# A GLA head's eight samples loaded, multiplied and normalised in one step instead of two of four

## The chip, the cores and the metric

One core of a Trainium2 chip runs the whole kernel. The metric is the device time of one execution in microseconds (us); lower is better. A core has five engines with a queue of instructions each: PE (matmul; its weight loads, PEld, overlap it), DVE (vector), ACT (scalar, activations), POOL and SP (here both mostly issue DMAs). An engine runs its queue in order, and waits on semaphores for the others.

## What is computed

The reference is one layer of a hybrid decoder: a gated linear recurrence (LRU) and gated linear attention (GLA) side by side, for a prompt of 2048 tokens and for eight samples of one token with states of their own. The change concerns the samples in GLA. For each of four heads, with a state `S` of 128 x 256 per sample:

```
S = exp(dl[:, :, 0, :])[..., None] * S + k^T v          # for one token
o = q S
o = o * lax.rsqrt(jnp.mean(o * o, axis=-1, keepdims=True) + EPS) * g_gla_norm
y_gla = o.reshape(Bn, T, D_GLA) * silu(zg)
```

The new states are an output, and `y_gla` goes, with the prompt's, into the output projection.

## The kernel before

The prompt is done in two halves of 1024 tokens; the second half carries the samples' eight columns as well. Within a half the heads follow in the order 3, 0, 1, 2. A head projects its values (matmuls L346 to L348, three for one product since operands are split in a high and a low part, and L661 to L663 for all other projections), then runs GLA over three segments of 384, 384 and 256 + 8 columns, in chunks of 128 tokens, and behind each head stands an LRU tile (L1315 to L1317 are its gates, with the convolution L1278 and the scan L1318 to L1334 around them).

A chunk of GLA goes like this. ACT rounds the transposed keys and the masked products (L1051 kTh, L1048 amh), DVE makes their low parts (L1052 kTl, L1049 aml). PE multiplies keys and values (L1068 to L1070, the last with kTl) and adds up the chunk's outputs in the one PSUM buffer po (L1072 to L1076). DVE copies them out (L1081), which frees po for the next L1072, and ACT sums their squares (L165). A segment's norm is a chain of small DVE steps (rsqrt, L147 to L153), then L1089 scales the outputs, L1162 transposes them on PE, and L1167 multiplies by gain and gate.

The samples of a head are done by `sample_state` and `sample_out`, four at a time. A group loads its value rows, copied to all 128 partitions (L1098), and its states (L1100), both issued from POOL into two buffers of 4 x 256 columns with the tag xt, of which there are just two. Per sample DVE puts the query into a zeroed tile (L1103 qm), ACT scales the state by the decay (L1104), and DVE adds key times value (L1105). Three units of work later PE multiplies the four queries by the four states (L1114: 32 rows of po for each sample), the states go out (L1115), and po is copied to the tile os (L1117). The second group, two units behind the first, needs the buffers of the first and so waits until its products are done; its products are added to os by DVE (L1119). Then follow the sum of squares, rsqrt, and the scale (L1124). The last segment's outputs for the samples are brought into place by L1164, beside L1162, which waits for L1124. `finish` holds that step back until the norm is in the program.

What stands where is not written by hand. Functions queue pieces of work with `after(units, fn)`; `tick()` counts units between pieces of projection and starts what is due. A scheduler then orders the instructions of each engine when the program is built, by its own estimates of time. On chip each engine follows that order.

Two raw buffers with the tag wr hold a head's unsplit value weights (`raw_values`, L333, on POOL), which L912 reads for the samples' values; near the end of the kernel two loads of another kind (L1960, SP) use them. A head's raw weights are read before its samples' states are loaded.

Of the kernel before, what the change touches and what calls it, by code (L numbers as in the profile page):

```python
# [8 lines left out]
F32 = mybir.dt.float32  # L9
F32R = mybir.dt.float32r  # L10
I32 = mybir.dt.int32
AF = mybir.ActivationFunctionType
OP = mybir.AluOpType

P = 128
# [4 lines left out]
NS = 8  # L20
H = 4
DK = 128
DV = 256
# [26 lines left out]
def dram(ap, off, pattern):  # L50
    return bass.AP(tensor=ap.tensor, offset=ap.offset + off, ap=pattern)
# [3 lines left out]
def hybrid_kernel(ctx, tc, i, o):  # L55
    nc = tc.nc
    V, S, G, PE, SP = nc.vector, nc.scalar, nc.gpsimd, nc.tensor, nc.sync
# [13 lines left out]
    vsd = dpool.tile([H, NS, DV], F32, tag="vsd", name="vsd")  # L71
# [11 lines left out]
    cp = p1.enter_context(tc.tile_pool(name="cp", bufs=1))  # L83
    hnp = p1.enter_context(tc.tile_pool(name="hnp", bufs=1))
    wp = p1.enter_context(tc.tile_pool(name="wp", bufs=2))
    xp = p1.enter_context(tc.tile_pool(name="xp", bufs=2))
# [22 lines left out]
    sc = cp.tile([P, KT, 32], F32, tag="sc", name="sc")  # L109
# [591 lines left out]
    def after(units, fn, gla=False, val=False):  # L701
        clock[1] += 1
        heapq.heappush(pend, (clock[0] + units, clock[1], fn, gla, val))
# [384 lines left out]
        for c in range(nch):  # L1088
            V.tensor_scalar(on[:, c], on[:, c], rs[:, c:c + 1], None, op0=OP.mult)  # L1089

    def sample_state(h, smp, b0, st, done):

        if b0 == 0:
            st[:] = [cp.tile([P, NS, 32], F32, tag="sc", name="qm"), gp.tile([P, DV], F32, tag="os", name="os")]
            V.memset(st[0], 0.0)
        qm = st[0]
        vb = xp.tile([P, 4, DV], F32, tag="xt", name="xt")
        G.dma_start(vb, dram(vsd, (h * NS + b0) * DV, [[0, P], [DV, 4], [1, DV]]))  # L1098
        s0 = xp.tile([P, 4, DV], F32, tag="xt", name="xt")
        G.dma_start(s0, i["state_gla"][0, b0:b0 + 4, h].rearrange("b k v -> k b v"))  # L1100
        for n in range(4):
            b = b0 + n
            V.tensor_copy(qm[:, b, b:b + 1], smp[:, 0, b:b + 1])  # L1103
            S.activation(s0[:, n], s0[:, n], AF.Copy, scale=smp[:, 2, b:b + 1])  # L1104
            V.scalar_tensor_tensor(s0[:, n], vb[:, n], smp[:, 1, b:b + 1], s0[:, n],  # L1105
                                   op0=OP.mult, op1=OP.add)
        after(3, lambda: sample_out(h, b0, st, s0, done), True)

    def sample_out(h, b0, st, s0, done):

        qm, os_ = st
        po = psum.tile([P, 512], F32, tag="o", name="po", bufs=1)[:, :DV]
        for n in (3, 0, 1, 2):
            PE.matmul(po[32 * n:32 * n + 32], qm[:, b0 + n], s0[:, n], start=True, stop=True)  # L1114
        G.dma_start(o[7][0, b0:b0 + 4, h].rearrange("b k v -> k b v"), s0)  # L1115
        if b0 == 0:
            V.tensor_copy(os_, po)  # L1117
            return
        V.tensor_tensor(os_, os_, po, op=OP.add)  # L1119
        ss = gp.tile([P, 4], F32, tag="oss2", name="oss2")  # L1120
        rs = gp.tile([P, 4], F32, tag="ors2", name="ors2")
        square_sum(xp, ss[:, :1], os_, P, DV)
        rsqrt(gp, rs[:, :1], ss[:, :1], 1, P, 1.0 / DV)
        V.tensor_scalar(os_, os_, rs[:, :1], None, op0=OP.mult)  # L1124
        done()

    def silu(z, ps):
        S.activation(z, ps, AF.Tanh, scale=0.5)  # L1128
# [41 lines left out]
    def gla_head(half, h, wv=None, ahead=None):  # L1170
# [4 lines left out]
        else:  # L1175
# [5 lines left out]
            v = values(half, h, w)  # L1181
            wk = weights(K0 + h * DK, DK)
            wq = weights(Q0 + h * DK, DK)
        prep, zs, os_, state = {}, {}, [None], []

        def chunks(s, c):

# [28 lines left out]
                return  # L1216
            gla_out(half, h, s, prep[s, "run"][1], os_[0] if s == 2 else None, [zs[s, 0], zs[s, 1]])

        def sample(smp, b0):
            sample_state(h, smp, b0, state, lambda: after(0.5, lambda: os_.__setitem__(0, state[1]), True))  # L1220

        pk = None
        if not wv:
# [18 lines left out]
                after(2 if h == HEADS[0] else 1, lambda: chunks(0, 0), True, True)  # L1242
            tick()
        if half == 1:
            after(1, lambda: sample(prep[2][3], 0), True)
            after(3, lambda: sample(prep[2][3], 4), True)
        if wv:
            modulate_samples(st, xsr)
            hn_sample()
# [807 lines left out]
    smp = {}  # L2057
# [201 lines left out]
```

## Time and profile before

| | us |
|---|---|
| three runs | 1453.64, 1453.55, 1456.39 (median 1453.64) |
| profiled execution | 1452.05 |
| its span | 1450.3 |
| L1104, one of 32 (ACT) | 0.50 |
| L1105, one of 32 (DVE) | 0.48 |
| L1114, landing of its states (L1100, median) | 5.9 |

The prediction quotes rows of the trace: start in us, duration in us, engine, line, operation, tiles (written tile <- read tiles), shape, and in brackets the idle time of that engine before the row with what ended it. A row with x2 or x4 covers that many instructions in a row (for the products, x8 counts the two passes of each). Rows of waits give engine, tile and line that waited, what it waited for, then us in total, times, and the longest. Line numbers are those of the kernel before, unless said otherwise.

### The profile page before, as it was taken

The numbers are of one execution on the slowest core, as the hardware profiler recorded it, in microseconds if no ns is written. First come the engines' busy times: TensorE is split into PE (matmuls) and PEld (weight loads), VectorE is DVE, ScalarE is ACT, GpSimd is POOL, SyncE is SP. The second block draws the span as 40 slices with busy tenths as digits, with TensorE's granted clock in tenths as the row PEclk, the third lists the DMA queues.
The fourth block names the chain that finished last, engine by engine and source line by source line (L and its number), as shares of the span: only waits on it lengthen the run. The fifth ranks groups of instructions, "written<-read, shape, count | busy, mean of one in ns | idle before, by whom it ended". The sixth has DMA issues, their size and how long they took to land. (4 is left out here: it accounts for less than half of the span.)

```text
span 1450.3 us, 23579 instructions
## 1 busy us (share of the span) xinstructions
PE 1425.6 (98%) x8741; PEld 1253.1 (86%) x8741; DVE 1051.2 (72%) x2477; ACT 690.0 (48%) x1251; POOL 220.5 (15%) x364
## 2 busy tenths in 40 slices
PE   8999999999999999999999999999999999999998
PEld 6888989899898988878999998999998887788886
DVE  5757658776676688955458687686888986688886
ACT  4644544662545358624354544535557522144342
POOL 0200111212122013100111321433210000000000
PEclk9999999999999999999999999999999999999999
DMA  9755775774665446667844665756672767694453
GB/s 329 267 185 175 259 264 196 251 243 156 200 217 192 160 175 213 204 224 236 293 153 154 201 205 163 244 188 203 213 256 77 279 223 273 229 361 135 135 173 116
DMA packets 161752, 305.33 MB, mean 211 GB/s; under 512 B 12962, under 2 KB 91458, under 8 KB 159197
## 3 DMA queue, kind: packets, MB, share of 16 engines
q1 hardware_dynamic: 106837, 217.39, 44.0%
q0 software_dynamic: 22752, 70.44, 14.3%
q10 hardware_dynamic: 32048, 16.00, 3.7%
q8 instruction: 69, 1.13, 0.3%
q14 instruction: 46, 0.38, 0.1%
HBM read 188.51 MB, written 115.33 MB: 210 GB/s over the span
## 5 line engine op out<-in xcount | busy, mean ns | idle before, releaser
L661 PE MATMUL acc<-hh,w 128*128 128x512 f32 (+3 forms) x1112 | 386.2, 347 | 1.3 <-DVE zs L1129 0.7
L663 PE MATMUL acc<-hh,w 128*128 128x512 f32 (+3 forms) x1112 | 375.6, 338 | 0.0
L662 PE MATMUL acc<-hl,w 128*128 128x512 f32 (+3 forms) x1112 | 375.3, 338 | 0.2 <-DVE hl L205 0.2
L661 PEld LDWEIGHTS acc<-hh,w 128*128 128x128 f32 x1112 | 209.3, 188 | 20.0 <-ACT tx L1318 0.9
L662 PEld LDWEIGHTS acc<-hl,w 128*128 128x128 f32 x1112 | 209.3, 188 | 17.2 <-DVE hl L205 0.5
L663 PEld LDWEIGHTS acc<-hh,w 128*128 128x128 f32 x1112 | 209.1, 188 | 16.8 <-issue 0.4
L1845 PE MATMUL acc<-w,a 128*128 128x512 f32 (+1 forms) x792 | 184.8, 386 | 0.0
L1845 PEld LDWEIGHTS acc<-w,a 128*128 128x128 f32 x792 | 146.8, 188 | 33.2 <-issue 3.4
L346 PE MATMUL acc<-w,hh 128*128 128x256 f32 (+1 forms) x508 | 144.9, 285 | 0.1
L347 PE MATMUL acc<-w,hh 128*128 128x256 f32 (+1 forms) x508 | 143.6, 283 | 0.0
L348 PE MATMUL acc<-w,hl 128*128 128x256 f32 (+1 forms) x508 | 143.6, 283 | 0.0
L1845 PE MATMUL tp<-w,a 128*128 128x512 f32 x564 | 136.0, 391 | 0.0
L1845 PEld LDWEIGHTS tp<-w,a 128*128 128x128 f32 x564 | 105.3, 188 | 26.8 <-issue 5.2
L346 PEld LDWEIGHTS acc<-w,hh 128*128 128x128 f32 x508 | 96.8, 191 | 1.3 <-ACT zs L1128 0.4
L348 PEld LDWEIGHTS acc<-w,hl 128*128 128x128 f32 x508 | 96.4, 190 | 0.0
L347 PEld LDWEIGHTS acc<-w,hh 128*128 128x128 f32 x508 | 95.9, 189 | 0.2
L1128 ACT ACTIVATE zs<-acc 128x512 f32<-128x512 f32 (+3 forms) x70 | 34.5, 492 | 107.4 <-PE acc L663 105.2
L1695 ACT CAST a<-s 128x512 fp32r<-128x512 f32 x61 | 36.5, 619 | 95.9 <-issue 36.6
L1278 DVE SCALAR_TENSOR_TENSOR cv<-xa,vecT,cv 128x512 f32<-128x512 f32 (+2 forms) x120 | 77.1, 645 | 6.0 <-ACT cv L1276 5.7
L1129 DVE SCALAR_TENSOR_TENSOR zs<-zs,acc 128x512 f32<-128x512 f32 (+3 forms) x70 | 38.6, 551 | 47.3 <-ACT zs L1128 47.2
L957 ACT CAST vh<-acc 128x256 fp32r<-128x256 f32 x56 | 20.5, 370 | 83.3 <-PE acc L348 70.0
L958 DVE TENSOR_TENSOR vl<-acc,vh 128x256 fp32r<-128x256 f32 x56 | 23.4, 420 | 43.1 <-ACT vh L957 43.0
(403 smaller groups left out, 2752.0 us busy)
## 6 DMA issues: line engine op xcount, KB each, us to landing
parts<-w SPq DMA_DIRECT2D x37, 1024.0 KB
w<-parts SPq DMA_DIRECT2D x28, 1024.0 KB
wr<-in_w_in_dram SPq DMA_DIRECT2D x38, 512.0 KB
a<-mixd SPq DMA_DIRECT2D x63, 256.0 KB
w<-wd SPq DMA_DIRECT2D x12, 1024.0 KB
w<-twd SPq DMA_DIRECT2D x20, 512.0 KB
mixd<-zs ACTq DMA_DIRECT2D x34, 256.0 KB
wada<-in_w_ada_dram SPq DMA_DIRECT2D x16, 512.0 KB
```

The source lines that it names most:

```text
L346: PE.matmul(ps, hh[:, kt, c], hi[:, kt % 4], start=kt == 0, stop=False)
L347: PE.matmul(ps, hh[:, kt, c], lo[:, kt % 4], start=False, stop=False)
L348: PE.matmul(ps, hl[:, kt, c], hi[:, kt % 4], start=False, stop=kt == KT - 1)
L661: PE.matmul(ps[:, :n], hi[:, kt], a, start=kt == 0, stop=False)
L662: PE.matmul(ps[:, :n], hi[:, kt], b, start=False, stop=False)
L663: PE.matmul(ps[:, :n], lo[:, kt], a, start=False, stop=kt == KT - 1)
L958: V.tensor_tensor(lo, ps[:, :DV], hi.bitcast(F32), op=OP.subtract)
L1128: S.activation(z, ps, AF.Tanh, scale=0.5)
L1129: V.scalar_tensor_tensor(z, z, 1.0, ps, op0=OP.add, op1=OP.mult)
L1278: V.scalar_tensor_tensor(cv[:, cq], xa[:, cq.start + k:cq.stop + k], cw[k], cv[:, cq], op0=OP.mult, op1=OP.add)
L1695: S.copy(t[:, 0, k], (low(t) if src is None else src)[:, k])
L1845: PE.matmul(ps, t[:, u, k], w[:, v, k, c], start=(q < 3 or ps is own) and (k, u, v) == (0, 0, 0), stop=(k, u) == (3, 1), skip_group_check= ...
```

## The change

`sample_state` is now called once per head, one unit behind the last segment's projections, and loads all eight samples: the first four into the xt buffers, the second four into the wr buffers. The scales of all eight follow each other. `sample_out` comes four units later (before: three, for each group) and multiplies all eight into one PSUM buffer: the first four start the sums, the second four add to them, which is the same as adding the two results since each product has rows of zeros for the other samples. One copy to os remains, the add is gone. The norm's end is told to `finish` as before, half a unit later.

```diff
@@ -1088,41 +1088,42 @@
         for c in range(nch):
             V.tensor_scalar(on[:, c], on[:, c], rs[:, c:c + 1], None, op0=OP.mult)
 
-    def sample_state(h, smp, b0, st, done):
-
-        if b0 == 0:
-            st[:] = [cp.tile([P, NS, 32], F32, tag="sc", name="qm"), gp.tile([P, DV], F32, tag="os", name="os")]
-            V.memset(st[0], 0.0)
-        qm = st[0]
-        vb = xp.tile([P, 4, DV], F32, tag="xt", name="xt")
-        G.dma_start(vb, dram(vsd, (h * NS + b0) * DV, [[0, P], [DV, 4], [1, DV]]))
-        s0 = xp.tile([P, 4, DV], F32, tag="xt", name="xt")
-        G.dma_start(s0, i["state_gla"][0, b0:b0 + 4, h].rearrange("b k v -> k b v"))
-        for n in range(4):
-            b = b0 + n
-            V.tensor_copy(qm[:, b, b:b + 1], smp[:, 0, b:b + 1])
-            S.activation(s0[:, n], s0[:, n], AF.Copy, scale=smp[:, 2, b:b + 1])
-            V.scalar_tensor_tensor(s0[:, n], vb[:, n], smp[:, 1, b:b + 1], s0[:, n],
-                                   op0=OP.mult, op1=OP.add)
-        after(3, lambda: sample_out(h, b0, st, s0, done), True)
-
-    def sample_out(h, b0, st, s0, done):
-
-        qm, os_ = st
+    def sample_state(h, smp, done):
+
+        qm = cp.tile([P, NS, 32], F32, tag="sc", name="qm")
+        V.memset(qm, 0.0)
+        s0 = []
+        for b0, pool, tag in ((0, xp, "xt"), (4, wp, "wr")):
+            vb, x = [pool.tile([P, 1088], F32, tag=tag, name=tag)[:, :4 * DV] if b0 else
+                     pool.tile([P, 4 * DV], F32, tag=tag, name=tag) for _ in range(2)]
+            vb, x = [y.rearrange("p (b v) -> p b v", v=DV) for y in (vb, x)]
+            G.dma_start(vb, dram(vsd, (h * NS + b0) * DV, [[0, P], [DV, 4], [1, DV]]))
+            G.dma_start(x, i["state_gla"][0, b0:b0 + 4, h].rearrange("b k v -> k b v"))
+            for n in range(4):
+                b = b0 + n
+                V.tensor_copy(qm[:, b, b:b + 1], smp[:, 0, b:b + 1])
+                S.activation(x[:, n], x[:, n], AF.Copy, scale=smp[:, 2, b:b + 1])
+                V.scalar_tensor_tensor(x[:, n], vb[:, n], smp[:, 1, b:b + 1], x[:, n],
+                                       op0=OP.mult, op1=OP.add)
+            s0.append(x)
+        after(4, lambda: sample_out(h, qm, s0, done), True)
+
+    def sample_out(h, qm, s0, done):
+
+        os_ = gp.tile([P, DV], F32, tag="os", name="os")
         po = psum.tile([P, 512], F32, tag="o", name="po", bufs=1)[:, :DV]
-        for n in (3, 0, 1, 2):
-            PE.matmul(po[32 * n:32 * n + 32], qm[:, b0 + n], s0[:, n], start=True, stop=True)
-        G.dma_start(o[7][0, b0:b0 + 4, h].rearrange("b k v -> k b v"), s0)
-        if b0 == 0:
-            V.tensor_copy(os_, po)
-            return
-        V.tensor_tensor(os_, os_, po, op=OP.add)
+        for m in range(2):
+            for n in (3, 0, 1, 2):
+                PE.matmul(po[32 * n:32 * n + 32], qm[:, 4 * m + n], s0[m][:, n], start=m == 0, stop=m == 1)
+        for m in range(2):
+            G.dma_start(o[7][0, 4 * m:4 * m + 4, h].rearrange("b k v -> k b v"), s0[m])
+        V.tensor_copy(os_, po)
         ss = gp.tile([P, 4], F32, tag="oss2", name="oss2")
         rs = gp.tile([P, 4], F32, tag="ors2", name="ors2")
         square_sum(xp, ss[:, :1], os_, P, DV)
         rsqrt(gp, rs[:, :1], ss[:, :1], 1, P, 1.0 / DV)
         V.tensor_scalar(os_, os_, rs[:, :1], None, op0=OP.mult)
-        done()
+        done(os_)
 
     def silu(z, ps):
         S.activation(z, ps, AF.Tanh, scale=0.5)
@@ -1181,7 +1182,7 @@
             v = values(half, h, w)
             wk = weights(K0 + h * DK, DK)
             wq = weights(Q0 + h * DK, DK)
-        prep, zs, os_, state = {}, {}, [None], []
+        prep, zs, os_ = {}, {}, [None]
 
         def chunks(s, c):
 
@@ -1216,8 +1217,8 @@
                 return
             gla_out(half, h, s, prep[s, "run"][1], os_[0] if s == 2 else None, [zs[s, 0], zs[s, 1]])
 
-        def sample(smp, b0):
-            sample_state(h, smp, b0, state, lambda: after(0.5, lambda: os_.__setitem__(0, state[1]), True))
+        def sample(smp):
+            sample_state(h, smp, lambda x: after(0.5, lambda: os_.__setitem__(0, x), True))
 
         pk = None
         if not wv:
@@ -1242,8 +1243,7 @@
                 after(2 if h == HEADS[0] else 1, lambda: chunks(0, 0), True, True)
             tick()
         if half == 1:
-            after(1, lambda: sample(prep[2][3], 0), True)
-            after(3, lambda: sample(prep[2][3], 4), True)
+            after(1, lambda: sample(prep[2][3]), True)
         if wv:
             modulate_samples(st, xsr)
             hn_sample()
```

In the changed kernel L1104 is L1105, L1105 is L1106, L1103 is L1104, L1114 is L1117, L1124 is L1125, and L1127 to L1245 move on by one (L1162 is L1163, L1164 is L1165, L1167 is L1168).

The new order shows in three places. First ACT in head 0, in the last segment's GLA, where the states of the first four (xt) were scaled. Before:

```order
L1011 ACTIVATE e<-xb 128x256
L1104 ACTIVATE xt<-xt,smp 128x256
L1012 ACTIVATE xb<-xb 128x256
L165 ACTIVATE junk,oss<-on 128x256
L1051 CAST kTh<-tp 128x384
L1048 CAST amh<-am 128x384
```

After, with wr the states of the second four:

```order
L1105 ACTIVATE xt<-xt,smp 128x256
L1012 ACTIVATE xb<-xb 128x256
L1105 ACTIVATE wr<-wr,smp 128x256 x4
L165 ACTIVATE junk,oss<-on 128x256
L1051 CAST kTh<-tp 128x384
L1048 CAST amh<-am 128x384
```

The four scales of the second group stand behind the exponential L1012 and ahead of the sum of squares and the two roundings of the chunk.

Second DVE in head 1, from the norm of the second segment (L1089) to the copy of a chunk's outputs (L1081). Before:

```order
L1089 TENSOR_SCALAR on<-on,ors 128x256 x3
L1103 COPY qm<-smp 128x1
L1105 SCALAR_TENSOR_TENSOR xt<-xt,smp 128x256
L1103 COPY qm<-smp 128x1 x4
L1167 SCALAR_TENSOR_TENSOR zs<-tp,gsc,zs 128x384
L1081 COPY on<-po 128x256
```

After:

```order
L1089 TENSOR_SCALAR on<-on,ors 128x256 x3
L1104 COPY qm<-smp 128x1 x2
L1106 SCALAR_TENSOR_TENSOR wr<-wr,smp 128x256
L1104 COPY qm<-smp 128x1
L1106 SCALAR_TENSOR_TENSOR wr<-wr,smp 128x256
L1104 COPY qm<-smp 128x1
L1106 SCALAR_TENSOR_TENSOR wr<-wr,smp 128x256
L1104 COPY qm<-smp 128x1
L1106 SCALAR_TENSOR_TENSOR wr<-wr,smp 128x256
L1168 SCALAR_TENSOR_TENSOR zs<-tp,gsc,zs 128x384
L1081 COPY on<-po 128x256
```

Four steps on the states of the second group stand there instead of one on the first.

Third PE in head 0, at the products and the LRU gates. Before, the second group of products:

```order
L661 MATMUL acc<-hh,w 128x264
L662 MATMUL acc<-hl,w 128x264
L663 MATMUL acc<-hh,w 128x264
L1114 MATMUL po<-xt,qm 32x256 x4
L1315 MATMUL acc<-xh,wg 128x264
L1316 MATMUL acc<-xl,wg 128x264
L1317 MATMUL acc<-xh,wg 128x264
```

After, the one place of all products, with the last 128x384 projections ahead of it:

```order
L661 MATMUL acc<-hh,w 128x384
L662 MATMUL acc<-hl,w 128x384
L663 MATMUL acc<-hh,w 128x384
L1117 MATMUL po<-xt,qm 32x256 x4
L1117 MATMUL po<-wr,qm 32x256 x4
L1315 MATMUL acc<-xh,wg 128x384
L1316 MATMUL acc<-xl,wg 128x384
L1317 MATMUL acc<-xh,wg 128x384
```

The products moved from behind the 128x264 projections of the head's last gate to ahead of them, and the group that stood among the 128x384 projections is gone.

## The prediction

> **What bounds the kernel now.** I read the busy times of the profile's page first, then PE's waits, then the granted clock by stretches around the longest wait, then the timelines of that place, engine by engine.
>
> ```profile
> PE 1425.6 (98%) x8741; PEld 1253.1 (86%) x8741; DVE 1051.2 (72%) x2477; ACT 690.0 (48%) x1251; POOL 220.5 (15%) x364
> ```
> ```profile
> PE po L1114 <- DVE xt L1105: 2.1, 1, 2.1
> PE acc L1315 <- DVE zs L1129: 1.4, 1, 1.4
> PE tp L1164 <- DVE os L1124: 0.8, 1, 0.8
> ```
>
> PE works 98% of the span, so only what takes work or a wait off PE counts, and any new wait of PE is paid in full. One of its longest waits is at the lines changed: L1114 waits once, 2.1 us, for the scaled states of L1105. The stretches around it (us, then PE, PEld, DVE, ACT, POOL busy, and the granted clock):
>
> ```profile
> 20.61:24.02 3.41, 1.47 (x32) 0.96 (x28) 2.19 (x7) 0.19 (x1) 0.00 (x0) 1.00 1.13 331
> 24.02:27.43 3.41, 3.41 (x36) 3.02 (x25) 1.88 (x5) 2.42 (x4) 0.61 (x1) 0.50 1.10 347
> ...
> 884.18:887.59 3.41, 1.29 (x15) 1.01 (x15) 1.68 (x4) 1.71 (x4) 0.00 (x0) 1.00 0.26 43
> 887.59:891.00 3.41, 3.41 (x21) 2.84 (x14) 1.95 (x4) 1.74 (x5) 0.77 (x1) 0.50 1.00 408
> ...
> 1109.00:1113.00 4.00, 2.63 (x15) 2.03 (x13) 4.00 (x14) 1.62 (x4) 0.14 (x1) 1.00 0.58 182
> ```
>
> The wait has a second price: the 3.41 us behind it run at half clock. It happens twice in the trace, after 1.94 us idle in 3.41 and after 2.12; 1.37 idle brought no drop. The cause of the wait, from the chain of work:
>
> ```profile
> 879.94 4.99 DMA xt<-in_state_gla_dram
> ...
> 885.01 0.52 ACT xt L1104
> ...
> 885.56 1.70 DVE xt L1105 x4
> ...
> 887.34 0.89 PE po L1114 x8
> ```
>
> In head 0 the states of samples 4 to 7 are requested only at 879.94 (their buffer is free once the first four's L1114 at 878.18 is done), land 5 us later, and are then scaled one by one.
>
> **The change, part by part.** All eight are loaded together and multiplied in one place.
>
> (a) *Head 0's wait.* PE there:
>
> ```profile
> 878.18 0.64 PE L1114 MATMUL po<-xt,qm 128*32 128x256 f32 x8
> 878.75 0.45 PE L663 MATMUL acc<-hh,w 128*128 128x384 f32 x1
> ...
> 884.94 0.28 PE L663 MATMUL acc<-hh,w 128*128 128x264 f32 x1
> 887.34 0.89 PE L1114 MATMUL po<-xt,qm 128*32 128x256 f32 x8 [2.12 <-DVE xt L1105]
> 888.16 0.59 PE L1315 MATMUL acc<-xh,wg 128*128 128x264 f32 x1
> ...
> 890.93 0.32 PE L346 MATMUL acc<-w,hh 128*128 128x256 f32 x1
> 891.09 0.28 PE L347 MATMUL acc<-w,hh 128*128 128x256 f32 x1
> ...
> 891.44 0.28 PE L347 MATMUL acc<-w,hh 128*128 128x256 f32 x1
> ```
>
> The group at 878.18 goes (0.57 to the next matmul); all eight products now stand ahead of the 128x384 L1315s, where the operands are some 20 us old. Eight in a row are not in the trace: they cost between one group (0.57) and two (1.14); I take 1.05, near two, because only the switch into the group is saved. So the L663 of 884.94 starts at 884.94 - 0.57 + 1.05 = 885.42, and L1315 at 885.54 instead of 888.16: **-2.62**. The twelve matmuls from 888.16 to 890.93 took 2.77; at the spacing after 891.09 (0.35 for three) they take 1.40: **-1.37**. Next in line is L1164 (the normalised outputs), and these are then ready 3 us ahead of it. Together -4.0.
>
> (b) *The scales of the second four.* They leave the places of 885.01 and its like and go to where the first four are scaled, inside a chunk of the prompt's GLA. ACT, DVE and PE there, head 0:
>
> ```profile
> 848.45 0.40 ACT L1012 ACTIVATE xb<-xb 128x256 f32<-128x256 f32 x1
> 849.89 0.42 ACT L165 ACTIVATE junk<-on 128x256 bf16<-128x256 f32 x1 [1.04 <-DVE on L1081]
> ```
> ```profile
> 850.50 0.15 DVE L147 TENSOR_SCALAR rs_x<-oss 128x3 f32<-128x3 f32 x1
> ...
> 850.90 0.55 DVE L1052 TENSOR_TENSOR kTl<-tp,kTh 128x384 fp32r<-128x384 f32 x1
> ```
> ```profile
> 851.19 0.28 PE L1069 MATMUL pkv<-vl,kTh 128*128 128x256 f32 x1
> 851.50 0.39 PE L1070 MATMUL pkv<-vh,kTl 128*128 128x256 f32 x1
> ```
>
> The four new scales stand behind L1012, ahead of L165. One of these or of DVE's L1105 follows another by 0.40 (four of L1105 took 1.70 in the chain, 0.48 of it the last), so the four scales need 1.60 where ACT idled 1.04: L165 and all behind it +0.57. DVE's L147 needs L165's sum, so it moves to 851.07; behind it now stands one L1105, 0.40, that stood behind L1052. L1052 goes from 850.90 to 851.64 (0.17 of smaller work between), **+0.74**. PE's L1070 starts 0.05 behind L1052's end already, so PE waits 0.74 longer. The timelines of heads 1 and 2 show the same rows at the same distances. In head 3 PE doesn't wait here, and I take nothing for it.
>
> The loads:
>
> ```profile
> 833.53 0.77 POOL L1100 DMA_DIRECT2D xt<-in_state_gla_dram  x1
> ```
>
> The second four's loads stand right behind this one and are first used at 848.9; the one of 879.94 took 4.99. They would have to take three times that to be waited for: nothing.
>
> (c) *DVE behind the norm.* In head 1 all four L1105s of the second four stand between L1089 and L1081. Before:
>
> ```profile
> 948.70 0.87 DVE L1089 TENSOR_SCALAR on<-on,ors 128x256 f32<-128x256 f32 x3
> 949.49 0.15 DVE L1103 COPY qm<-smp 128x1 f32<-128x1 f32 x1
> ...
> 949.95 0.33 DVE L1103 COPY qm<-smp 128x1 f32<-128x1 f32 x4
> 950.21 0.62 DVE L1167 SCALAR_TENSOR_TENSOR zs<-tp,gsc,zs 128x384 f32<-128x384 f32 x1
> 950.74 0.41 DVE L1081 COPY on<-po 128x256 f32<-128x256 f32 x1
> ```
> ```profile
> 951.21 0.38 PE L1072 MATMUL po<-vh,amh 128*128 128x256 f32 x1
> ```
>
> 0.72 us from 949.49 to 950.21 become 4 x 0.40 + 5 x 0.07 = 1.95, so L1081 ends 0.74 + 1.23 later, at 953.1, and PE's L1072, which has followed it by 0.06, starts 1.96 later, of which 0.35 is work moved ahead of it: +0.83 on top of (b). In heads 0 and 2 such work fills a gap that DVE has there anyway (if it doesn't, that is the second rival). Head 3:
>
> ```profile
> 770.74 0.56 DVE L1303 TENSOR_TENSOR xl<-cv,xh 128x384 fp32r<-128x384 f32 x1 [0.58 <-ACT xh L1302]
> 772.43 0.62 DVE L1167 SCALAR_TENSOR_TENSOR zs<-tp,gsc,zs 128x384 f32<-128x384 f32 x1 [1.14 <-PE tp L1162]
> 772.97 0.41 DVE L1081 COPY on<-po 128x256 f32<-128x256 f32 x1
> ```
>
> The rest of the added work, about 2.05 by then, meets gaps of 0.58 and 1.14: L1081 some +0.33, and L1072, the next matmul on that buffer, waits as much.
>
> (d) *The norm's place.* In head 3 L1164 stands 17 of the next head's value matmuls sooner, 17 x 0.117 = 2.0 us, but the norm is not 2.0 sooner: the products are one unit sooner and the add is gone, yet DVE's row of small steps has the prompt's norm and LRU work among it as before. Ends: 0, and 2.0 if the norm is no sooner at all; I take +0.5. In head 2:
>
> ```profile
> 1073.11 0.35 DVE L1124 TENSOR_SCALAR os<-os,ors 128x256 f32<-128x256 f32 x1
> ```
>
> PE waits 0.8 for this L1124 today. L1164 moves ahead there as well, by 19 matmuls, and the products by a unit, which leaves half the wait: -0.4 (from -0.8 to +0.8). One group of L1114 in the middle of the transposes goes too, 0.4 of its 0.57, since its four now ride on another group: -0.8 together.
>
> (e) *The rest.* Joined groups save 0.1 each in heads 3 and 1 (0 to 0.57, as in (a)). Behind head 2's products DVE's four L1105 and ACT's four L1104 are no longer in the LRU's chain; the waits of 1.1 to 1.4 us further on (the L1315 of the second fence) can shrink: I take -0.5, between 0 and the 1.1 of one of them. POOL's queue loses its waits for PE's first products. The next head's second raw weight load (L333) now stands behind the state's output and waits for the products, in head 0 at 881; it is read here:
>
> ```profile
> 913.65 0.57 PE L912 MATMUL acc<-wr,fs 128*8 128x64 f32 x27
> ```
>
> 32 us are room for a load of 5. On SP one L1960 now waits for head 2's products, which stand between their two places of today; behind it stands:
>
> ```profile
> 1064.80 0.33 SPq L1367 DMA_DIRECT2D wg<-parts x1
> ```
>
> which waits for PE until then anyway, and PE's waits name none of these loads: nothing. DMA bytes are the same.
>
> **Sum.** Head 3: 0.33 + 0.5 - 0.1 = +0.7. Head 0: 0.74 - 4.0 = -3.3. Head 1: 0.74 + 0.83 - 0.1 = +1.5. Head 2: 0.74 - 0.8 = -0.1. Tail -0.5. In all 0.7 - 3.3 + 1.5 - 0.1 - 0.5 = **-1.7**. The profiled execution took 1452.05 (span 1450.3), so 1450.4; the median of the runs, 1453.64, is 1.6 above that execution, so the forecast for the median is **1452.0**, a little less than before.
>
> [...]
>
> **Rivals.**
> - *All gain, new work hidden.* If the scheduler's neighbours leave DVE and ACT room where I count 0.33 to 0.83, (b) to (d) cost 0.3 a head at most: -4.0 + 1.2 - 0.8 - 0.4 - 1.1 = -5.1, 1448.5. For it: DVE is busy 72%, ACT 48%. Against: L1070 and L1072 follow their operands by 0.05 now. 0.31.
> - *Slower: the extra DVE work is paid in every head.* If the shift of 1.6 in head 1 comes in all four, that is +6.4 - 4.0 - 0.2 = +2.2; and where its two parts fall within one 3.41 us window (from about 1.5 us idle), a half-clock stretch adds 1.4: +3.6, 1457.2. Against: the parts are 8 us apart in head 1. 0.16.
> - *The change doesn't do what it says.* The half clock comes anyway, from shorter waits in one window, or the moved L1164 takes over as much: -1.7 + 1.4 = -0.3, 1453.3. Against: around 885 no other wait stands in the trace. 0.10.
> - *My forecast*, 1452.0 with 1450 to 1454 of its own: 0.43.
>
> The measurement tells 0.2% (2.9 us) from no change. Faster is the first rival and the lower edge of the forecast, 0.36; slower is the second, 0.16; the rest 0.48. The range: from 1448.0 (the full gain and 0.5) to 1456.3 (most of the second).
>
> **What would show it.** PE's wait at the products of head 0 gone and the clock 1.00 around 885 to 891 (a); L1070 some 0.7 longer behind L1069 in heads 0, 1 and 2 (b); L1072 waiting for L1081 0.8 in head 1 and 0.3 in head 3 (c); a wait at L1164 (L1165 of the changed kernel) of 0.5 in head 3 and less than 0.8 in head 2 (d); shorter waits at L1315 near the end (e). Wrong it would be if a second four landed late, or if a new half-clock stretch stood anywhere.

## The result, and the profile after

| | before | after |
|---|---|---|
| median of six runs each, us | 1453.60 | 1447.89 |
| lowest to highest | 1452.19 to 1456.39 | 1446.87 to 1449.76 |
| profiled execution | 1452.05 | 1449.01 |
| its span | 1450.3 | 1447.2 |

The ratio is 0.9963 (95% interval 0.9953 to 0.9973): 5.4 us less (3.9 to 6.8), a gain above the 0.2% that can be told from no change. The forecast of 1452.0 had the sign and the place of the largest gain, and a third of the size; the time lies 0.1 below the low end of the range and 0.6 from the first rival's 1448.5.

Each step had a place at which it would show. Step (a), PE at head 0's products, from the timeline of after (start, duration, line, tiles, shape, count), and the stretches around it (us; PE, PEld, DVE, ACT, POOL busy; granted clock; DMA share; GB/s):

```profile
882.04 0.64 PE L1117 MATMUL po<-xt,qm 128*32 128x256 f32 x8
882.50 0.61 PE L1117 MATMUL po<-wr,qm 128*32 128x256 f32 x8
883.04 0.44 PE L1315 MATMUL acc<-xh,wg 128*128 128x384 f32 x1
```
```profile
881.40:884.80 3.40, 3.40 (x33) 2.56 (x31) 2.53 (x10) 1.42 (x4) 0.78 (x2) 1.00 0.38 121
884.80:888.20 3.40, 3.40 (x31) 3.40 (x30) 2.30 (x14) 1.13 (x5) 0.00 (x0) 1.00 0.51 154
888.20:891.60 3.40, 3.40 (x32) 3.40 (x32) 1.63 (x3) 3.32 (x5) 0.00 (x0) 1.00 0.89 283
```

The wait is gone, PE is busy in every part of these ten us, and the clock is 1.00 in each. All eight products take 1.00 us (883.04 - 882.04), where the working had 1.05.

Step (b), ACT, DVE and PE in head 0's last segment of GLA:

```profile
849.57 0.40 ACT L1012 ACTIVATE xb<-xb 128x256 f32<-128x256 f32 x1
849.88 1.69 ACT L1105 ACTIVATE wr<-wr,smp 128x256 f32<-128x256 f32 x4
851.48 0.40 ACT L165 ACTIVATE junk<-on 128x256 bf16<-128x256 f32 x1
```
```profile
852.00 0.17 DVE L147 TENSOR_SCALAR rs_x<-oss 128x3 f32<-128x3 f32 x1
852.08 0.48 DVE L1106 SCALAR_TENSOR_TENSOR xt<-xt,smp 128x256 f32<-128x256 f32 x1
852.55 0.55 DVE L1052 TENSOR_TENSOR kTl<-tp,kTh 128x384 fp32r<-128x384 f32 x1
```
```profile
852.61 0.28 PE L1069 MATMUL pkv<-vl,kTh 128*128 128x256 f32 x1
853.15 0.38 PE L1070 MATMUL pkv<-vh,kTl 128*128 128x256 f32 x1 [0.27 <-DVE kTl L1052]
```

L1070 starts 0.54 behind L1069, where it was 0.31: the wait is there, but a third of the 0.74. L1068 and L1069 come a little late as well: from the last projection's matmul to L1072 PE takes 1.15 (852.22 to 853.37) where before took 0.78 (850.95 to 851.73), so the place costs 0.37. Steps (c), (d) and (e) in PE's waits (tile and line, what it waited for; us in total, times, longest):

```profile
PE acc L661 <- DMA w<-parts: 1.8, 2, 1.3
...
PE acc L1315 <- DVE zs L1130: 1.4, 1, 1.4
...
PE po L1072 <- DVE on L1081: 0.9, 2, 0.7
...
PE pkv L1070 <- DVE kTl L1052: 0.8, 3, 0.3
PE tp L1165 <- DVE os L1125: 0.7, 2, 0.4
```

L1072 waits 0.70 in head 1 (forecast 0.83) and not in head 3 (0.33). The second of the two at L1072 is 0.25 in head 0, where the second execution of after has none and one of before 0.20. L1165 waits 0.33 in head 3 (0.5) and 0.39 in head 2 (0.4 left of 0.8). The wait of 1.4 at L1315 stands as before. Another one a little ahead of it, which before has in this row, is gone:

```profile
PE acc L1315 <- ACT tx L1318: 1.1, 1, 1.1
```

The first row of after's is larger than in before (0.3): L661 waits for a projection's weights at the start of heads 0 and 1. A second profiled execution of before, below, shows the same wait with 2.2 us, so it is not of the change.

What the rows add up to shows best by heads. PE's first L912 of a head is a mark that both kernels have; here in after:

```profile
732.30 1.13 PE L912 MATMUL acc<-wr,fs 128*8 128x68 f32 x64
...
820.67 1.08 PE L912 MATMUL acc<-wr,fs 128*8 128x64 f32 x64
...
910.61 1.08 PE L912 MATMUL acc<-wr,fs 128*8 128x64 f32 x64
...
1000.71 1.08 PE L912 MATMUL acc<-wr,fs 128*8 128x64 f32 x64
```

From mark to mark, in us, in two profiled executions of each kernel (the second ones are from the experiments), the last column to the start of PE's last matmul:

| | head 3 | head 0 | head 1 | head 2 and all behind |
|---|---|---|---|---|
| before | 88.70, 88.69 | 93.09, 93.99 | 89.03, 89.62 | 440.70, 441.34 |
| after | 88.37, 88.35 | 89.93, 89.52 | 90.10, 90.23 | 439.63, 439.35 |
| difference of the means | -0.34 | -3.8 | +0.8 | -1.5 |
| forecast | +0.7 | -3.3 | +1.5 | -0.6 |

The sum is -4.8, inside the interval of the runs. The two profiled executions of the first table differ by 3.0 only (1452.05 and 1449.01): before's lies 1.6 under its median, after's 1.1 above.

### The profile page after: what moved, and what is told of

Its sections match the earlier page's. It is cut to its first block, busy times and chain, and to the rows that moved or that the text cites. A ratio compares the mean times of both kernels' runs of the same rounds, so it can differ in the third digit from the quotient of the medians.

```text
span 1447.2 us, 23571 instructions
## 1 busy us (share of the span) xinstructions
PE 1420.5 (98%) x8741; PEld 1248.7 (86%) x8741; DVE 1049.8 (73%) x2473; ACT 690.2 (48%) x1251; POOL 219.4 (15%) x364
## 5 line engine op out<-in xcount | busy, mean ns | idle before, releaser
L661 PE MATMUL acc<-hh,w 128*128 128x512 f32 (+3 forms) x1112 | 385.7, 347 | 3.0 <-DMA w<-parts 1.8
L661 PEld LDWEIGHTS acc<-hh,w 128*128 128x128 f32 x1112 | 209.2, 188 | 21.7 <-DVE f L1005 1.6
L346 PE MATMUL acc<-w,hh 128*128 128x256 f32 (+1 forms) x508 | 143.8, 283 | 0.1
L346 PEld LDWEIGHTS acc<-w,hh 128*128 128x128 f32 x508 | 95.6, 188 | 1.3 <-ACT zs L1129 0.4
```

What stands on the lines that cost most here:

```text
L346: PE.matmul(ps, hh[:, kt, c], hi[:, kt % 4], start=kt == 0, stop=False)
L661: PE.matmul(ps[:, :n], hi[:, kt], a, start=kt == 0, stop=False)
```

## The experiments

Theory A, after the result: nearly all of the gain is head 0's late load, so that the second pair of buffers alone, with two groups and the add as before, brings two thirds or more of it. Its rival: the buffers bring little by themselves, and the rest of the rewrite (one place for the scales, joined products, a norm one unit sooner) brings most. Ratios are to the kernel before, run on the same chip; they are turned into us on 1453.6.

### The changed kernel again

No edit.

> The changed kernel once more, nothing edited. Its first trace has a wait of 1.29 us at the L661 of 826.3 for a weight load (w<-parts) and one of 0.53 at 916.2, where before had 0.3 in all. If the change causes them (its loads crowd that load), they stand here too, within 0.3 us; if they are chance of that one execution, they are gone or smaller by half, and the span is shorter by as much. Against before: 4.5 to 6.5 us faster, by the interval already measured.

Measured: 1447.91, ratio 0.9963 (0.9951 to 0.9975), -5.4 us. The gain holds in a second set of runs.

### The buffers alone

Before, with the second four in the wr buffers; units, groups and add stay.

```diff
-        vb = xp.tile([P, 4, DV], F32, tag="xt", name="xt")
+        vb, s0 = [wp.tile([P, 1088], F32, tag="wr", name="wr")[:, :4 * DV].rearrange("p (b v) -> p b v", v=DV) if b0 else
+                  xp.tile([P, 4, DV], F32, tag="xt", name="xt") for _ in range(2)]
...
-        s0 = xp.tile([P, 4, DV], F32, tag="xt", name="xt")
```

> Before, with only the buffers changed: the second four in the raw weights' buffers; products stay in two groups with the add, the norm stays where it was. Theory A (the late load of the second four is the cost): head 0's wait and its half clock go (-4.0), the wait of 1.1 at L1315 near the end goes (-1.1), the scales crowd the chunk (+0.5 in heads 0, 1 and 2): about -3.6 to -4.8 against before, so at least two thirds of the change. Rival B (the joined products and the earlier norm make the gain): -2.0 or less.

Measured: 1452.41, ratio 0.9993 (0.9984 to 1.0002), -1.0 us (-2.3 to +0.3). Theory A falls: it asked for -3.6 to -4.8. PE's waits of this kernel show what stands against the gain:

```profile
PE acc L661 <- DVE S L1056: 2.0, 1, 2.0
...
PE tp L1164 <- DVE stT L1339: 1.2, 1, 1.2
...
PE acc L1315 <- ACT tx L1318: 0.4, 1, 0.4
```

Head 0 gains 3.0 in its trace (90.50). Near the end the wait at L1315 falls from 1.1 to 0.4, but the one at L1164 for the samples' outputs grows from 0.8 to 1.2, and the time from head 2's mark on, 440.69, is that of before (440.70 and 441.34). The wait of 2.0 at L661 falls into head 1 (93.44), at the place where other traces wait for the weights; the row names DVE's L1056 as the last to be ready, but in head 1 of the other traces that wait there L661 starts 1.1 to 1.8 before L1056 ends, so it doesn't need it. The mean granted clock of this execution is 0.995, where the one with head 0's buffers only has 0.997, and with 1455.20 it is the slowest of the eleven, so head 1's loss need not be in the others.

The wait at L1164 has its cause in DVE's order in head 2:

```profile
1076.53 1.23 DVE L1331 SCALAR_TENSOR_TENSOR tg<-xl,tg 128x1032 f32<-128x1032 f32 x1
...
1077.80 1.23 DVE L1332 TENSOR_TENSOR tx<-tx,tg 128x1032 f32<-128x1032 f32 x1
...
1079.02 0.61 DVE L1278 SCALAR_TENSOR_TENSOR cv<-xa,vecT,cv 128x384 f32<-128x384 f32 x1
1079.54 2.35 DVE L1334 TENSOR_TENSOR_SCAN tg<-xl,hc,tx 128x1024 f32<-128x1024 f32 x1
...
1081.86 0.35 DVE L1124 TENSOR_SCALAR os<-os,ors 128x256 f32<-128x256 f32 x1
```

The norm's last two small steps are at 1077.68 and 1078.95, between these: the scheduler put four long steps of the LRU into the norm's chain. L1164 starts 0.06 behind the end of L1124; the row of waits names L1339, which DVE does next. From head 2's mark L1124 starts at 76.0, where before has it at 70.4. So the edit didn't leave the norm where it was.

### The buffers in one head

The same edit with `if b0 and h == 0`, and with `if b0 and h == 2`.

> As the run with the buffers alone, but for head 0 only; heads 3, 1 and 2 as before. Theory A: the wait of 2.1 us and the 3.4 us of half clock behind it go, -4.0, and the crowded chunk of head 0 costs 0.5 to 0.8: -3.2 to -3.5 against before, the trace without a stretch at clock 0.50 near 888. Rival C (the half clock comes from something else and stays): -1.5 to -2.1, with the stretch at 0.50 still there.

> As the run with the buffers alone, but for head 2 only, where PE had no long wait for the second four. Theory A: ACT's and DVE's scales leave the chain of the LRU behind them, so the wait of 1.1 us at L1315 (1092.2 before) goes, at +0.5 for the crowded chunk: -0.4 to -1.0 against before, the wait at 887 with its half clock unchanged. Rival D (that wait belongs to the LRU's own latency): +0.3 to +0.6, the wait at L1315 still 1.0 or more.

Measured: head 0 only 1451.54, ratio 0.9989 (0.9979 to 0.9999), -1.6 us (-3.1 to -0.1). Head 2 only 1454.35, ratio 1.0011 (1.0001 to 1.0022), +1.6 us (0.1 to 3.2). The waits of the second:

```profile
PE po L1114 <- DVE xt L1105: 2.6, 1, 2.6
...
PE tp L1164 <- DVE stT L1339: 1.2, 1, 1.2
```

In the first, the trace has neither head 0's wait nor half clock behind it (granted clock 1.00 from 885 to 920), and head 0 takes 90.52, 3.0 less than before's mean; the runs gain half of that. In the second, head 0 keeps its wait, 2.6 this time, and head 2 changes one wait for another as in the run above, with the LRU's steps in the norm's chain again. Its time from head 2's mark on is 440.46, no more than before's, so the loss of the runs shows in no row there. Head 0's buffers bring a little, and head 2's no gain in this order.

### Head 0's wait taken away in the kernel before

Two kernels that leave out work, with all else as before. The first leaves out, in head 0, the decay and the update of the second four's states (L1104, L1105), so that only their load can be waited for; the second leaves out only the decay of these four (L1104).

```diff
-            S.activation(s0[:, n], s0[:, n], AF.Copy, scale=smp[:, 2, b:b + 1])
-            V.scalar_tensor_tensor(s0[:, n], vb[:, n], smp[:, 1, b:b + 1], s0[:, n],
-                                   op0=OP.mult, op1=OP.add)
+            if not (h == 0 and b0):
+                S.activation(s0[:, n], s0[:, n], AF.Copy, scale=smp[:, 2, b:b + 1])
+                V.scalar_tensor_tensor(s0[:, n], vb[:, n], smp[:, 1, b:b + 1], s0[:, n],
+                                       op0=OP.mult, op1=OP.add)
```

> Before, where head 0's second four are neither scaled by the decay nor given key times value (their outputs and new states are the raw states' products): nothing is moved, only the work between the states' landing and the products is gone. Theory A: PE's wait falls from 2.1 to at most 0.2 and no half clock follows, -3.0 to -3.8 against before; this is the price of head 0's wait without any crowding elsewhere. Rival C (half clock of another cause): -1.5 to -2.1, with a stretch at 0.50 near 888.

> Before, where head 0's second four are not scaled by the decay (ACT's four L1104 left out, DVE's four L1105 stay): DVE starts at the landing, so PE's wait falls by 0.5 to 1.5 - 1.7. This asks where the clock gate decides, between 1.37 us idle (no drop) and 1.94 (a drop): with a drop the run is 0.4 to 0.6 faster than before, without one 1.7 to 2.1 faster, and the stretch behind the wait is at 0.50 or at 1.00.

Measured: without both 1449.91, ratio 0.9985 (0.9976 to 0.9994), -2.2 us (-3.5 to -0.9); without the decay 1452.31, ratio 0.9996 (0.9987 to 1.0005), -0.6 us (-1.9 to +0.7). In the first kernel's trace the wait is gone, the mean granted clock is 0.998 (0.997 and 0.996 in before's two traces), and head 0 takes 89.29; with the weights' wait at L661 taken off (0.28 here, 0.30 and 1.68 in before's two traces) that is 3.5 less than before's mean, the 2.1 and 1.4 of the wait and its half clock. The runs gain less, 3.5 at most.

In the second kernel the wait was expected to fall and didn't. The states' load is issued later, as POOL's row of issues shows:

```profile
881.61 0.55 POOL L1211 DMA_DIRECT2D zs<-zgd  x1 [3.22 <-DVE rs_y L153]
882.15 0.55 POOL L1205 DMA_DIRECT2D out_dram<-S  x1
882.81 0.76 POOL L1100 DMA_DIRECT2D xt<-in_state_gla_dram  x1
```

The first products are done at 880.28, but POOL waits until 881.61 before it issues a load of the gate, and the states' load is the second behind that. In before's first trace the same three stand at 878.74, 879.28 and 879.94, with the products done at 878.82. So it isn't only the buffer that makes head 0's load late, it is also what stands ahead of it on POOL. The trace tells something of the clock too:

```profile
888.96 0.64 PE L1115 MATMUL po<-xt,qm 128*32 128x256 f32 x8 [2.27 <-DVE xt L1106]
```
```profile
884.25:887.66 3.41, 2.43 (x21) 2.22 (x19) 0.92 (x3) 0.80 (x2) 0.00 (x0) 1.00 0.57 154
887.66:891.08 3.42, 2.12 (x21) 1.74 (x22) 2.26 (x7) 0.89 (x4) 0.78 (x1) 1.00 0.89 295
891.08:894.49 3.41, 3.41 (x33) 3.41 (x32) 2.99 (x15) 3.33 (x5) 0.00 (x0) 1.00 0.64 243
```

2.27 us of waiting, 0.15 more than before's 2.12, and no half clock behind it. The bounds of these stretches are those at which the clock changes in this trace, carried on by 3.413 us, the length of both stretches at half clock that the prediction shows of before's trace. So split, which is an estimate, the wait leaves 0.98 idle in one (3.41 less 2.43 busy) and 1.30 in the next (3.42 less 2.12). In the kernel with head 2's buffers only, bounds found in the same way leave 1.81 of the wait in one stretch (3.41 less 1.60 busy), and half clock follows:

```profile
889.34:892.75 3.41, 1.60 (x16) 1.22 (x17) 2.38 (x6) 1.54 (x4) 0.77 (x1) 1.00 0.82 263
892.75:896.17 3.42, 3.42 (x18) 3.42 (x17) 2.88 (x12) 3.35 (x6) 0.00 (x0) 0.50 0.76 274
```

So the second price of head 0's wait, -1.37 in step (a), doesn't fall due in each execution: behind 2.27 here it didn't, behind 2.12 in before and 2.6 with head 2's buffers only it did. That the lie of the wait in these stretches decides it is an estimate from these two splits.

### The products one unit later, and one sooner

```diff
-        after(4, lambda: sample_out(h, qm, s0, done), True)
+        after(5, lambda: sample_out(h, qm, s0, done), True)
```

and the same with 3.

> The changed kernel with sample_out five units behind the loads, where the last of before's products stood: the products stay joined, the norm is as late as before. Theory A2 (the earlier norm is worth its place): in head 2 PE waits again for the norm (0.8 to 1.2 at L1165 instead of 0.4) and the waits near the end come back in part: +0.7 to +1.7 against the changed kernel, -3.5 to -5.0 against before. Rival E (only the joining counts): within 0.3 of the changed kernel, -5.0 to -6.0 against before.

> The changed kernel with sample_out three units behind the loads instead of four. If the norm still is what PE waits for at L1165 (0.33 in head 3, 0.39 in head 2), a unit more takes both away: -0.5 to -0.9 against the changed kernel, 0.9957 to 0.996 against before. Rival: the products then come among other work and the norm's small DVE steps crowd GLA: 0 to +1, 0.9963 to 0.997.

Measured: five units 1449.60, ratio 0.9980 (0.9972 to 0.9989), -2.9 us (-4.1 to -1.6); three units 1451.43, ratio 0.9986 (0.9977 to 0.9996), -2.0 us (-3.3 to -0.6). Both keep less than the -5.4 of four, three units by more than either expectation allowed. PE's waits from 1000 to 1120 us that differ, head 2 and the start of what follows, of after, of five units and of three:

```profile
PE tp L1165 <- DVE os L1125: 0.4, 1, 0.4
```
```profile
PE tp L1165 <- DVE stT L1339: 1.3, 1, 1.3
PE acc L1315 <- ACT tx L1318: 0.6, 1, 0.6
```
```profile
PE acc L661 <- DMA w<-parts: 0.8, 1, 0.8
PE acc L1315 <- ACT tx L1318: 0.5, 1, 0.5
```

With five units DVE's order has the LRU's steps inside the norm's chain, as with the buffers alone: L1125 starts 75.2 behind head 2's mark (66.7 in after), L1165 waits 1.3 for it, and the LRU's L1315 waits 0.6. With three the norm is in time, but L1315 waits 0.5 and L661 0.8 for weights. From head 2's mark to the end it is 440.59 and 440.60, 1.1 more than after's 439.49; of three units' 1.1 the weights are 0.8, a wait that comes and goes. The kernels with the products at four units and early loads have 438.7 to 439.6 there (four traces), and before and the kernels made from it 440.5 to 441.3 (seven). At four units the norm's chain stands whole ahead of L1331 to L1334 and ends 3.7 us sooner than in before; at five it is split and ends 4.7 us later. So this pair of runs compares two orders on DVE, and not one unit more or less with all else equal.

The rest of the difference is partly in the choice of execution. Heads 3, 0 and 1 together are 267.94 and 267.92, no more than after's two traces with 268.41 and 268.10, but those two hold 1.8 and 1.6 of waits for weights at L661, and five units' 0.5 and three units' none. With these waits taken off, from head 3's mark to PE's last matmul, before has 711.2 and 711.4, after 706.2 and 705.9, five units 708.0 and three 707.7: -5.3, -3.3 and -3.6, where the runs have -5.4, -2.9 and -2.0. What three units lose beyond that shows in no row.

### The second four's loads, or their scales alone, later

Both start from after. One lets the loads of the second four and their scales follow half a unit later, behind DVE's work of that time; the other loads early, as after does, and lets only the scales follow later, behind ACT's.

```diff
-            G.dma_start(vb, dram(vsd, (h * NS + b0) * DV, [[0, P], [DV, 4], [1, DV]]))
-            G.dma_start(x, i["state_gla"][0, b0:b0 + 4, h].rearrange("b k v -> k b v"))
-            for n in range(4):
...
+            def four(b0=b0, vb=vb, x=x):
+                with held(V) if b0 else ExitStack():
+                    G.dma_start(vb, dram(vsd, (h * NS + b0) * DV, [[0, P], [DV, 4], [1, DV]]))
+                    G.dma_start(x, i["state_gla"][0, b0:b0 + 4, h].rearrange("b k v -> k b v"))
+                for n in range(4):
...
+            after(0.5, four, True) if b0 else four()
```

In the other, the two loads stay where they are, and `with behind(S)` stands around the loop.

> The changed kernel with the second four's loads held back half a unit behind DVE's work, so that ACT's and DVE's scales of the second four leave the chunk of the first four and stand about 8 us later, products still joined and at four units. Theory A: the waits of 0.27 at L1070 in three heads and 0.7 at L1072 in head 1 go: -1.5 to -2.2 against the changed kernel, -7 to -8 against before. Rival F (the same work costs PE as much at the new place, or the later load lands late): -4.5 to -6 against before, with waits of 0.3 to 0.7 at other lines.

> The changed kernel, its loads as early as there, but the second four's scales (ACT and DVE) are kept behind the first four's chunk in program order, half a unit later; products joined at four units as there. Theory A: the waits of 0.27 at L1070 (0.5 a head with the smaller delays beside them) in heads 0, 1 and 2 and 0.7 at L1072 in head 1 go: -1.0 to -2.2 against the changed kernel, so a ratio of 0.9948 to 0.9957 against before. Rival F (they cost PE as much behind the chunk, since they now stand ahead of the rounding of the next chunk): within 0.5 of the changed kernel, 0.996 to 0.9967.

Measured: loads later 1463.62, ratio 1.0080 (1.0067 to 1.0093), +11.6 us. Its longest waits:

```profile
PE po L1122 <- DVE wr L1109: 5.1, 2, 4.3
PE tp L1170 <- DVE os L1130: 3.1, 2, 2.6
```

The products (L1122 here) wait 4.3 for the second four in head 0, and head 2 waits 2.6 for its norm: a second four that is loaded late costs more than all that the change gains. With joined products, then, early loads are a condition of the gain, though by themselves not the gain.

Scales later, with early loads: 1447.95, ratio 0.9963 (0.9949 to 0.9976), -5.4 us, just after's. Its waits at L1070 and the one at L1072 in head 1 are gone, with 0.3 at L1072 and 0.5 at L346 in head 0; by the marks it is 1.9 faster than after's mean (89.18, 89.77, 87.99 and 438.85), about as much as after's two traces wait for weights, of which this one shows nothing. The runs show no gain. What the crowding of (b) and (c) costs is less than these runs tell apart.

### The kernel before, profiled again

No edit.

> Before once more, nothing edited, for a second trace. What the clock gate does should hang on where the wait of head 0 falls: the half-clock stretches seen so far all lie on a grid of 3.413 us of their own execution and follow a stretch of that grid with 1.75 us or more of PE idle, never one with 1.51 or less (past the first 15 us). So here: a wait of 2.0 to 2.6 at the second products of head 0; half clock behind it only if at least 1.7 of it lies in one stretch of the grid. If half clock follows a wait that is split more evenly, the grid is wrong.

Measured: 1454.94, span 1453.2. Its waits have the row at L661 that was larger in after, and head 0's wait (2.2) has its half clock, behind a stretch with 1.95 of PE idle (3.41 less 1.46 busy):

```profile
PE po L1114 <- DVE xt L1105: 2.2, 1, 2.2
...
PE acc L661 <- DMA w<-parts: 2.2, 2, 1.7
...
PE tp L1164 <- DVE os L1124: 0.9, 1, 0.9
...
PE acc L1315 <- ACT tx L1318: 0.9, 1, 0.9
```
```profile
885.90:889.31 3.41, 1.46 (x13) 1.25 (x11) 1.51 (x4) 1.71 (x4) 0.00 (x0) 1.00 0.30 55
889.31:892.72 3.41, 3.14 (x17) 2.36 (x18) 1.41 (x4) 1.06 (x4) 0.78 (x1) 0.50 0.95 383
```

The long waits of head 0 and of the end are of the kernel, the one for the weights comes and goes: 0.3 for head 0 in the first execution, 1.7 in this one.

### The second four's scales left out

After, leaving out the decay and the update of the second four's states in all heads.

```diff
+                if b0:
+                    continue
                 S.activation(x[:, n], x[:, n], AF.Copy, scale=smp[:, 2, b:b + 1])
```

> The changed kernel where the second four of every head are neither scaled by the decay nor given key times value (their outputs and new states come from the raw states): the loads, the joined products and the norm stay where they are, only the work that crowds the chunk is gone. It prices what the change still pays. Theory A: the waits at L1070 (0.5 a head in three heads with the delays beside them) and L1072 (0.7 in head 1) go, -1.5 to -2.5 against the changed kernel, 0.9945 to 0.9953 against before. Rival G (PE's gains are given back at the weight loads, L661 on w<-parts, which vary from run to run): within 0.7 of the changed kernel, 0.9958 to 0.9968, with 1.5 us or more of those waits in the trace.

Measured: 1446.95, ratio 0.9956 (0.9942 to 0.9969), -6.4 us. That is 1.0 under after, with overlapping intervals: the second four's scales, all of (b) and (c), cost after some 1 us, and the run can't tell that from nothing. It lies between the expectations, -1.5 or more and 0.7 at most. By the marks its trace is 3.1 under after's mean, 0.8 of it by shorter waits at L661.

## Why the prediction was right in sign and short in size

The runs part the gain of 5.4 in three. The buffers alone: -1.0 (-2.3 to +0.3). Scales, products and norm joined, but the products five units behind: -2.9, so 1.9 more, with intervals that overlap. The products at four units: -5.4, so 2.5 more, with intervals that just touch. The prediction's sum had nearly all its gain in head 0's wait. The parts are those of these kernels and not of single causes, since each edit also changes the scheduler's order.

**(a), head 0's wait: right as a mechanism, and what the prediction gave as one price holds for some executions.** The wait and the half clock are gone, and both traces of before pay them (93.09 and 93.99; 89.7 after). But where this is taken away in the kernel before, the runs gain 1.6 with the new buffers in head 0 (at most 3.1, the sum had 3.3 for it) and 2.2 with the work left out (at most 3.5, which is what the wait and the half clock come to). The working also put the late load down to the buffer alone; the loads ahead of it on POOL delay it too. The granted clock of the single executions says the same of the second term: its mean is 0.9966 in 79 of before and 0.9978 in 12 of after; one stretch of 3.41 us at half clock takes 3.41 x 0.5 / 1450 = 0.0012 off it, so before has on the mean one such stretch more, wherever it lies. At equal clock, 0.998, seventeen executions of before have a mean of 1452.1 and six of after 1447.9: some 4 of the 5.4 us are there at equal clock.

**(b), +0.74 in heads 0, 1 and 2: failed in size.** PE waits 0.27 at L1070 in each, and head 0's place costs 0.37 in all. DVE's part came out: L1052 starts 0.55 behind L147, the working had 0.57. Two other steps didn't. "L165 and all behind it +0.57" was too much: from L1012 to L147 it is 2.43 where it was 2.05, so +0.38. And the working let ACT and PE keep their distance, while L1012 now stands 2.65 ahead of PE's last projection there (849.57 and 852.22), 0.15 more than before (848.45 and 850.95). **(c), +0.83 and +0.33: right in place for head 1** (0.70), wrong for head 3, where no wait is. (By its own rows the first is 1.96 - 0.35 - 0.74 = 0.87.) With the weights' wait taken off (0.53 and 0.67 in after's traces, none and 0.52 in before's), head 1 grew by 0.5, not by 1.5.

**(d), the norm's place: right.** +0.5 in head 3 is there as 0.33, and in head 2 0.39 of 0.8 is left where 0.4 was forecast. Five units and the buffers alone show what the working left out: the norm's chain on DVE can be split by the LRU's steps, and then ends some 5 us later.

**(e), the rest: too small.** Joined groups were put at 0.1 a head. In head 3 seven traces without joined groups have 88.68 to 88.73, and three with them, after's two and five units, 88.35 to 88.37; but three others with joined groups, three units, scales later and scales left out, have 88.85 to 89.18. So what the joining itself saves is not shown. In head 0 traces with the buffers alone have 90.50 and 90.52, those of after 89.93 and 89.52. The tail was put at -0.5: the L1315 that waited 1.1 and 0.9 for ACT's L1318 waits no more, which is the working's far end. The step that failed is to take half of it and to count the norm's -0.4 apart from it: with the buffers alone, one of these two waits grows as the other falls, and after has both gains.

So the miss of some 3 us on the sum is 1.0 in head 3, 0.5 in head 0, 0.7 in head 1 and 0.9 from head 2 on. The waits that were added came out below their price, and the one at L1315 that was to stay in half is gone. In head 3 some 0.7 is in no wait: the head got 0.34 shorter though L1165 waits 0.33; where that comes from is open.

**The rivals.** The first, new work hidden, gave the size, and half its reason: L1070 and L1165 wait under 0.4 each, head 1 lost more. The second fell: no head but head 1 grew, and no stretch in after's trace went to half clock between the first 15 us and the last matmul. Its "from about 1.5 us idle" lies between the 1.37 and the 1.94 of before's trace and was an estimate; with three units the clock stayed at 1.00 behind 1.67. The prediction's row of 1109 to 1113 has a single wait of 1.37 (at L1315), so it says nothing of several short ones. In the third, the half clock that comes anyway was wrong for after, while "a moved wait takes over as much" is what the buffers alone do in head 2.

Open: what three units lose beyond their rows, and why the kernels without head 0's wait gain less in the runs than in their traces. Both traces of before pay the half clock (0.50 from 887.59 and from 889.31), and by the mean clock not each execution does, so the traces may overstate it; that is not shown execution by execution. Single executions of before scatter over 7 us, more than each of these terms.

## What to carry to other kernels

A wait that goes pays only if what stands next on the same engine is early enough too: the buffers alone turned one wait near the end into another (L1315 from 1.1 to 0.4, L1164 from 0.8 to 1.2), and the full gain came only where the norm's chain also ended ahead of the LRU's long steps. An edit to code that a scheduler orders is not one change: look at the new order of each engine before the time is put down to the edit. A trace is one execution; where terms of 1 us decide, two traces of the kernel before show which waits are its own and which come and go. Delays that the working carried from engine to engine came out at or below their price at all places here (0.27 for 0.74 at L1070, 0.70 for 0.83 at L1072 in head 1, none for 0.33 in head 3).

## What the runs showed of the hardware

In before's trace both stretches at half clock between the first 15 us and PE's last matmul last 3.413 us (24.02 to 27.43 and 887.59 to 891.00). With the second four's loads later the clock is 0.50 for 6.83 us, from 886.59 to 893.42. Ahead of the half clock stands a stretch of 3.41 us at full clock with 1.94 and 2.12 us of PE idle in before, 1.95 in before profiled again, 1.81 with head 2's buffers only, and 2.80 with the loads later. There the second half of the 6.83 follows 1.51 us of idle, at half clock already, so what was put ahead of before's second trace, that all of them follow 1.75 or more, is too wide. Without half clock behind it, the most idle in a stretch of that length, between the same bounds, is 1.37 in before and 1.35 in after, counted in steps of 3.413 us from the drops; with three units it is 1.67 in this one:

```profile
20.10:23.51 3.41, 1.74 (x37) 1.25 (x36) 2.99 (x14) 0.00 (x0) 0.00 (x0) 1.00 1.12 352
23.51:26.92 3.41, 3.02 (x47) 2.36 (x46) 1.96 (x5) 1.99 (x4) 0.61 (x1) 1.00 1.07 300
```

3.41 less 1.74 busy is 1.67 idle, and the clock stays at 1.00. So in these rows half clock follows 1.81 us of idle or more in a stretch at full clock and doesn't follow 1.67 or less; what comes between the two they don't show. In the trace without the decay, the wait of 2.27, split in 0.98 and 1.30 by the estimate above, has none behind it.

A load for a projection (w<-parts) is waited for at the start of a head for a time that changes from one execution of the same kernel to the next: 0.3 and 1.7 us at head 0 in the two of before, 1.3 and 0.9 in the two of after. The row of the 0.9 names DVE's L1002, which happened to end then; in before L661 starts at 826.47, ahead of L1002's end at 826.97, and so doesn't wait for it.
